# Strassen's scheme for a feed-forward up-projection, with a down-projection stage of its own

## The chip, the core and the metric

The kernel runs on one core of one Trainium2 chip. The metric is device time in microseconds (us) of one execution; the kernel before was timed three times: 2954.31, 2956.09 and 2958.66 us, median 2956.09.

## The reference

One layer of a streaming encoder on 512 tokens of width 2048, in float32. A mixer (a gated delta rule and a gated short convolution, between an input and an output projection) is followed by cross-attention into 256 memory tokens and by the feed-forward block that the change rewrites:

```python
def conv_ffn(h, w_up, conv_w, w_down):
    u = causal_dwconv(h @ w_up, conv_w)          # width 3, over tokens
    gate, up = u[..., :D_FF], u[..., D_FF:]      # D_FF = 5632
    return (jax.nn.silu(gate) * up) @ w_down
...
        h = rmsnorm(x, ffn_norm[l])
        x = x + conv_ffn(h, w_ffn_up[l], ffn_conv[l], w_ffn_down[l])
    return rmsnorm(x, final_norm)
```

## The kernel before, in words

Activations lie transposed: a tile of type T is [128 features, 512 tokens], and 16 of them hold one copy of the width. Every product of two float32 matrices is made of three matmuls (`mm3`, lines 149 to 152): each factor is split into a high and a low part of 12 significant bits in fp32r, and high x high, high x low and low x high are accumulated in PSUM. `wpiece` (line 131) loads a [128, 1024] piece of weights by SyncE's queue (tile wst, line 136), makes the high part on ScalarE (whi, line 139) and the low part on VectorE (wlo, line 140). `split` (lines 145 and 146) does the same for activations.

The stages follow one another: memory projections, mixer, attention scores, then `out_proj` (line 692), which brings attention's result back and adds it to the residual. There, tile by tile, ScalarE and GpSimd sum the squares for the norm, and the residual times the norm's gain is split into the high and low parts x2h and x2l (lines 710 and 711). The norm's factor of each token (`r2`) is applied after the up-projection, on its results.

The feed-forward block takes the 5632 hidden features in 11 chunks of 4 tiles (`FC`). For each of the 44 hidden tiles, `ffn_up` runs two projections (gate and up) of 16 k-tiles x 3 matmuls of 512 columns, multiplies by `r2` (line 729), does the convolution (lines 732 and 734), the Silu (736) and the product (737), and splits the result. `ffn_down` of the chunk before then adds this chunk's share of the down-projection to the residual tiles x2, which stay on chip (line 750). The last chunk goes through `ffn_down_last` in two halves of 256 tokens (line 766), each half with its final norm (lines 220, 211 to 216), its outputs (lines 782 to 785) and stores (787).

The order of instructions on each engine is not that of the program: a planner lets each engine take the earliest instruction of the program that it expects to be ready, and gives out the buffers of the pools. On the chip each engine then runs its instructions in that fixed order and waits on semaphores. Pools: `tp` (66 tiles of T), `wp` (3 wst, 4 whi, 4 wlo), `psm` and `psg` (3 and 5 banks of PSUM).

Of the kernel before, what the change touches and what calls it, by code (L numbers as in the profile page):

```python
# [15 lines left out]
P = 128  # L16
# [51 lines left out]
def trunk(ctx: ExitStack, tc: tile.TileContext, g):  # L68
    nc = tc.nc
    cpool = ctx.enter_context(tc.tile_pool(name="cpool", bufs=1))  # L70
    tp = ctx.enter_context(tc.tile_pool(name="tp", bufs=66))
    wp = ctx.enter_context(tc.tile_pool(name="wp", bufs=4))
# [10 lines left out]
    y_d = dpool.tile([H, P, S], F32, tag="y_d", name="y_d")  # L83
    gc_d = dpool.tile([4, H, P], F32, tag="gc_d", name="gc_d")
# [44 lines left out]
    def wpiece(src):  # L129
        """One [128, 1024] piece of weights, split into two parts of 12 significant bits."""  # L130
        st = wp.tile([P, 1024], F32, tag="wst", name=nm("wst"), bufs=3)
        shape = list(src.shape)
        stv = st
        if len(shape) == 3:
            stv = st.rearrange("p (a b) -> p a b", a=shape[1])
        nc.sync.dma_start(stv, src)
        hi = wp.tile([P, 1024], F32R, tag="whi", name=nm("whi"))
        lo = wp.tile([P, 1024], F32R, tag="wlo", name=nm("wlo"))
        nc.scalar.copy(hi, st)  # L139
        nc.vector.tensor_tensor(lo, st, f(hi), op=ALU.subtract)  # L140
        return hi, lo
# [40 lines left out]
    # the projections' pieces of weights, in order, split one piece ahead of their use  # L182
# [18 lines left out]
    def rsqrt(ms, ps, scale, bias):  # L201
        """1 / sqrt(ms), with one Newton step; ms = scale ps + bias is [128, n] in SBUF."""
# [20 lines left out]
    def rstd_rows(accs):  # L223
        """The norm's factor of each token, on every partition, from the sums of squares."""
# [43 lines left out]
    def mem_proj(w, then=None):  # L268
        """Projection of the normed memory, [hd, m], as two exact parts, two tiles of hd at a time."""
# [41 lines left out]
    # b and a of every head, the weights' two parts side by side  # L311
# [87 lines left out]
    def conv(ps, acc, c, taps):  # L399
        """Causal depthwise convolution over tokens, straight from PSUM."""  # L400
# [28 lines left out]
    def delta(h, q, k, v, z):  # L429
        q4, k4, v4_ = v4(q), v4(k), v4(v)  # L430
        # decays
# [12 lines left out]
        # k, tokens on partitions, and its norms: bk = beta / |k|^2, nk = |k|  # L444
# [17 lines left out]
        # k k^T and k q^T of each chunk  # L462
# [16 lines left out]
        # inverse of the unit triangular matrix: blocks of 32 by substitution,  # L479
        # a few columns of one block on each partition  # L480
# [36 lines left out]
        # then by blocks of doubling size: bt the inverse, pt its transpose  # L517
# [21 lines left out]
        # the scan over chunks  # L539
# [27 lines left out]
        # output norm (q's own norm is in it) and gate  # L567
# [72 lines left out]
    def turn():  # L640
        """The last softmax tiles, memory on partitions, as two exact parts."""
# [44 lines left out]
    x2, x2p = [], []  # L686
    x2s = []

    def out_proj(n, part):
        if part == 0:  # L690
            x2s.append((PM("psx2"), *wpiece(mo_d[:, :, n * P : (n + 1) * P].rearrange("k p n -> p k n"))))
        ps, hi, lo = x2s[n]
# [3 lines left out]
    for n in range(2):  # L696
        out_proj(n, 0)
    turn()
    for n in range(KT):
        if n >= 2:  # L700
            out_proj(n, 0)
        out_proj(n, 1)
        ps = x2s[n][0]
        x1 = T("x2")
        nc.sync.dma_start(x1, x1_d[n])
        nc.vector.tensor_tensor(x1, ps, x1, op=ALU.add)
        add_squares(acc2, x1, n == 0)
        th, tl = T("x2h", F32R), T("x2l", F32R)
        c = col(C_FFNN + n)
        nc.scalar.activation(th, x1, AF.Identity, scale=c)  # L710
        nc.vector.scalar_tensor_tensor(tl, x1, c, f(th), op0=ALU.mult, op1=ALU.subtract)
        x2.append(x1)
        x2p.append((th, tl))

# [1 line left out]
    r2 = []  # L716
    acc3 = cpool.tile([P, S], F32, tag="macc", name="acc3")

    def ffn_up(c):
        out = []  # L720
        for i in range(FC * c, FC * c + FC):
            us = []
            for t in (i, NF + i):
                ps = PM("psu")
                proj(lambda i2: g["w_up"][t, i2], x2p, ps)
                if not r2:
                    r2.append(rstd_rows([acc2]))
                u = T("u")
                nc.vector.tensor_tensor(u, ps, r2[0], op=ALU.mult)  # L729
                cv = T("ucv")  # L730
                cc = C_FCONV + 3 * t
                nc.scalar.activation(cv, u, AF.Identity, scale=col(cc + 2))
                for a in (1, 2):
                    nc.vector.scalar_tensor_tensor(cv[:, a:], u[:, : S - a], col(cc + 2 - a), cv[:, a:], op0=ALU.mult, op1=ALU.add)
                us.append(cv)
            nc.scalar.activation(us[0], us[0], AF.Silu)
            nc.vector.tensor_tensor(us[0], us[0], us[1], op=ALU.mult)
            out.append(split(us[0], "hd"))
        return out

    def ffn_down(c, hid):
        for n2 in range(KT // 2):
            hi, lo = wpiece(g["w_dn"][c, n2])
            for q in range(2):
                n = 2 * n2 + q
                ps = PG("psd")
                for k in range(FC):
                    o = k * 2 * P + q * P
                    mm3(ps, hi[:, o : o + P], lo[:, o : o + P], hid[k][0], hid[k][1], k == 0, k == FC - 1)
                nc.vector.tensor_tensor(x2[n], ps, x2[n], op=ALU.add)  # L750

    def ffn_down_last(c, hid):
        """The last part, the tokens in two halves, and the last norm of each."""
        S2 = S // 2
        for half in range(2):
            ts = slice(half * S2, (half + 1) * S2)
            for n2 in range(KT // 2):
                hi, lo = wpiece(g["w_dn"][c, n2])
                for q in range(2):
                    n = 2 * n2 + q  # L760
                    ps = PG("psd")[:, :S2]
                    for k in range(FC):
                        o = k * 2 * P + q * P
                        mm3(ps, hi[:, o : o + P], lo[:, o : o + P], hid[k][0][:, ts], hid[k][1][:, ts], k == 0, k == FC - 1)
                    xn = x2[n][:, ts]
                    nc.vector.tensor_tensor(xn, ps, xn, op=ALU.add)  # L766
                    if n == KT - 1:
                        last = T("sq")[:, :S2]
                        nc.scalar.activation(last, xn, AF.Square)
                    else:  # L770
                        add_squares(acc3[:, ts], xn, n == 0)
            r3 = rstd_rows([acc3[:, ts], last])
            if half == 0:
                nc.scalar.activation(cst[:, 3:4], r3[:, 0:1], AF.Ln)
            for n in range(KT):
                if n % 2 == 0:
                    o2 = T("o")
                o = o2[:, (n % 2) * S2 : (n % 2 + 1) * S2]
                xn = x2[n][:, ts]
                c2 = col(C_FINN + n)  # L780
                if n in (1, 4, 7, 9, 12, 14):
                    nc.scalar.activation(xn, xn, AF.Identity, scale=c2)
                    nc.gpsimd.tensor_tensor(o, xn, r3, op=ALU.mult)
                else:
                    nc.vector.scalar_tensor_tensor(o, xn, c2, r3, op0=ALU.mult, op1=ALU.mult)  # L785
                if n % 2:
                    nc.sync.dma_start(g["out"][n - 1 : n + 1, :, ts].rearrange("k p s -> p k s"), o2.rearrange("p (k s) -> p k s", k=2))

    prev = None
    for c in range(NF // FC):  # L790
        hid = ffn_up(c)
        if prev is not None:
            ffn_down(c - 1, prev)
        prev = hid
    ffn_down_last(NF // FC - 1, prev)


# [54 lines left out]
```

## Time and profile before

| What | Value |
|---|---|
| median of three executions | 2956.09 us |
| span of the profiled execution | 2963.6 us |
| TensorE, time in matmuls | 2901.9 us, 14497 matmuls |
| VectorE busy | 1551.5 us |
| ScalarE busy | 1053.6 us |
| GpSimd busy | 187.3 us |
| moved by the DMA engines | 365.42 MB, mean 123 GB/s |
| attention's output projection ends, up-projection begins | about 1500 us |

PE stands for TensorE, PEld for its weight loads, DVE for VectorE, ACT for ScalarE, POOL for GpSimd and SP for SyncE; L140 is line 140 of the kernel. A group's row gives engine, operation, output <- inputs with shapes, count, then busy time in us, mean duration in ns, and the engine's idle time just ahead of the group with what ended it. A row of stretches gives, from one time to another, each engine's busy time with its instructions, then the granted clock, the DMA engines' mean share and GB/s. A row of the timeline gives start and duration in us. A row of DMA issues ends with KB and the median us from issue to landing; a row of a DMA queue gives packets, MB and its packets' time as a share of 16 engines' span. Matmuls are pipelined, so what one costs is the distance from its start to the next one's.

### The profile page before, as it was taken

How to read it: one execution, taken by the hardware profiler on the slowest of the kernel's cores; microseconds unless marked ns; L12 is line 12 of the kernel's file. 1: busy time of each engine (PE TensorE's matmuls, PEld its weight loads, DVE VectorE, ACT ScalarE, POOL GpSimd, SP SyncE). 2: the span in 40 equal slices, each digit the busy share in tenths (PEclk: the TensorE clock that was granted, in tenths of full speed). 3: DMA queues.
4: the chain of work that ended last, by engine and by line, in shares of the span. 5: the costliest groups of instructions: out<-in, count | busy, mean ns of one | idle time of the engine just before them, and what ended most of it. 6: DMA issues, size and time to landing. Idle time of an engine off the chain costs nothing. (4 is left out here: it accounts for less than half of the span.)

```text
span 2963.6 us, 36108 instructions
## 1 busy us (share of the span) xinstructions
PE 2901.9 (98%) x14497; PEld 2437.6 (82%) x14497; DVE 1551.5 (52%) x2280; ACT 1053.6 (36%) x1427; POOL 187.3 (6%) x169
## 2 busy tenths in 40 slices
PE   7999999999999999999999999999999999999997
PEld 7999878777778888888888888888888888888887
DVE  5435747776664234446654544445454544444446
ACT  5454644444333223235443222223222232322225
POOL 1020001111110000110100000000000000000005
PEclk9999999999899999999999999999999999999999
DMA  6686763332232324446433333333333333333234
GB/s 201 214 287 199 237 192 107 89 96 82 82 96 87 100 94 152 148 147 185 143 113 94 99 99 93 100 95 97 100 93 99 98 94 100 94 98 100 93 100 135
DMA packets 143239, 365.42 MB, mean 123 GB/s; under 512 B 21200, under 2 KB 45152, under 8 KB 143072
## 3 DMA queue, kind: packets, MB, share of 16 engines
q1 hardware_dynamic: 129728, 337.93, 37.1%
q10 hardware_dynamic: 11392, 18.88, 1.7%
q0 software_dynamic: 1952, 6.31, 1.2%
q8 instruction: 113, 1.85, 0.2%
q14 instruction: 54, 0.44, 0.0%
HBM read 334.74 MB, written 28.33 MB: 123 GB/s over the span
## 5 line engine op out<-in xcount | busy, mean ns | idle before, releaser
L139 ACT CAST whi<-wst 128x1024 fp32r<-128x1024 f32 x592 | 622.1, 1052 | 1362.8 <-PE psu L151 472.9
L140 DVE TENSOR_TENSOR wlo<-wst,whi 128x1024 fp32r<-128x1024 f32 x592 | 726.2, 1228 | 601.3 <-ACT whi L139 577.7
L150 PE MATMUL psu<-x2h,whi 128*128 128x512 f32 x1408 | 548.1, 389 | 0.0
L152 PE MATMUL psu<-x2h,wlo 128*128 128x512 f32 x1408 | 547.7, 389 | 0.0
L151 PE MATMUL psu<-x2l,whi 128*128 128x512 f32 x1408 | 547.7, 389 | 0.0
L150 PEld LDWEIGHTS psu<-x2h,whi 128*128 128x128 f32 x1408 | 264.4, 188 | 55.1 <-issue 0.2
L151 PEld LDWEIGHTS psu<-x2l,whi 128*128 128x128 f32 x1408 | 264.4, 188 | 55.0 <-issue 0.2
L152 PEld LDWEIGHTS psu<-x2h,wlo 128*128 128x128 f32 x1408 | 264.3, 188 | 54.7
L150 PE MATMUL psd<-hdh,whi 128*128 128x512 f32 (+1 forms) x768 | 286.1, 373 | 2.7 <-DVE x L766 2.7
L152 PE MATMUL psd<-hdh,wlo 128*128 128x512 f32 (+1 forms) x768 | 286.2, 373 | 0.0
L151 PE MATMUL psd<-hdl,whi 128*128 128x512 f32 (+1 forms) x768 | 285.8, 372 | 0.0
L729 DVE TENSOR_TENSOR u<-psu,rsy 128x512 f32<-128x512 f32 x88 | 60.9, 692 | 288.8 <-PE psu L152 288.8
L750 DVE TENSOR_TENSOR x<-psd,x 128x512 f32<-128x512 f32 x160 | 110.7, 692 | 189.4 <-PE psd L152 189.4
L237 POOL TENSOR_TENSOR acc<-acc,sq 128x512 f32<-128x512 f32 (+1 forms) x58 | 73.4, 1266 | 1899.5 <-ACT sq L236 1898.3
L150 PEld LDWEIGHTS psd<-hdh,whi 128*128 128x128 f32 x768 | 145.4, 189 | 27.9 <-DVE x L766 2.9
L152 PEld LDWEIGHTS psd<-hdh,wlo 128*128 128x128 f32 x768 | 145.4, 189 | 25.0
L151 PEld LDWEIGHTS psd<-hdl,whi 128*128 128x128 f32 x768 | 145.4, 189 | 25.0
L150 PE MATMUL psq<-hh,whi 128*128 128x512 f32 x384 | 161.0, 419 | 0.0
L150 PE MATMUL psk<-mwh,whi 128*128 128x256 f32 x512 | 146.7, 286 | 12.5 <-ACT mwh L255 11.7
L151 PE MATMUL psq<-hl,whi 128*128 128x512 f32 x384 | 157.0, 409 | 0.0
L152 PE MATMUL psq<-hh,wlo 128*128 128x512 f32 x384 | 156.8, 408 | 0.0
L150 PE MATMUL pssc<-hh,whi 128*128 128x512 f32 x384 | 153.0, 398 | 0.0
(256 smaller groups left out, 4588.3 us busy)
## 6 DMA issues: line engine op xcount, KB each, us to landing
wst<-in_w_up SPq DMA_DIRECT2D x176, 512.0 KB, 3.5
wst<-in_w_mix SPq DMA_DIRECT2D x112, 512.0 KB, 3.6
wst<-in_w_dn SPq DMA_DIRECT2D x96, 512.0 KB, 3.5
wst<-in_w_xk SPq DMA_DIRECT2D x32, 512.0 KB, 3.6
wst<-in_w_xq SPq DMA_DIRECT2D x32, 512.0 KB, 4.5
wst<-in_w_xv SPq DMA_DIRECT2D x32, 512.0 KB, 4.3
wst<-in_w_xo SPq DMA_DIRECT2D x32, 512.0 KB, 4.7
wst<-in_w_mo SPq DMA_DIRECT2D x32, 512.0 KB, 3.6
```

The source lines that it names most:

```text
L139: nc.scalar.copy(hi, st)
L140: nc.vector.tensor_tensor(lo, st, f(hi), op=ALU.subtract)
L150: nc.tensor.matmul(ps, wh, xh, start=first, stop=False)
L151: nc.tensor.matmul(ps, wh, xl, start=False, stop=False)
L152: nc.tensor.matmul(ps, wl, xh, start=False, stop=last)
L237: nc.gpsimd.tensor_tensor(acc, acc, sq, op=ALU.add)
L729: nc.vector.tensor_tensor(u, ps, r2[0], op=ALU.mult)
L750: nc.vector.tensor_tensor(x2[n], ps, x2[n], op=ALU.add)
```

## The change

The up-projection is no longer 88 independent projections. For hidden tile i, the weights form a 2 x 2 block matrix: rows gate and up, columns the first and second half of the 2048 inputs (`w11`, `w12`, `w21`, `w22`, each [128, 1024]). The activations form another: the halves of the inputs by the halves of the tokens. One level of Strassen's scheme (with Winograd's sums) forms the four result blocks from 7 products of half-sized blocks in place of 8. The activations' sums are formed once, from pairs of residual tiles (n, n + 8) during the attention's output projection (`up_prepare`), and split: 7 operands of 8 k-tiles, 56 tiles of T. The weights' four sums are formed anew in each of the 44 units: `s1` and `s3` by accumulating DMAs from GpSimd's queue, `s2` and the last one on VectorE. PSUM accumulates px over products 1, 6, 7 and 4, and reads it out in between.

The residual x2 and the hidden tiles go through DRAM (`x2_d`, `hid_d`, written from ScalarE's queue). The down-projection follows as a stage of its own: four groups of four output tiles, each accumulating all chunks in PSUM, with the hidden tiles loaded and split again in each group. The last group leaves its last chunk out and does it in two halves of 256 tokens, with the final norm as before. Pools: `tp` 64 tiles, wst 5, whi and wlo 3 each; 7 residual work tiles (`tb`), whose place the 4 tiles of weight sums (`us`) take afterwards. The core of the diff:

```diff
+    def up_prepare(k, xa, xb):
+        tt = nc.vector.tensor_tensor
+        tc_, td = TB("tc"), TB("td")
+        tt(tc_[:, LO], xa[:, HI], xa[:, LO], op=ALU.subtract)
+        tt(tc_[:, HI], xb[:, HI], tc_[:, LO], op=ALU.subtract)
+        tt(td[:, LO], xa[:, HI], xb[:, HI], op=ALU.subtract)
+        tt(td[:, HI], xb[:, LO], tc_[:, HI], op=ALU.subtract)
...
+        for t, left, right in ((xb, 2, 3), (tc_, 5, 6), (td, 7, 4)):
+            th, tl = split(t, "xo")
+            xop[left].append((th[:, LO], tl[:, LO]))
+            xop[right].append((th[:, HI], tl[:, HI]))
...
+    for i in range(NF):
+        w11, w12, w21, w22 = (g["w_up"][q] for q in ((i, 0), (i, 1), (NF + i, 0), (NF + i, 1)))
+        s1 = us.tile([P, 1024], F32, tag="us", name=nm("s1"))
+        nc.sync.dma_start(s1, w21)
+        nc.gpsimd.dma_start(s1, w22, accum_op=ALU.add)
+        a11, a22, a12 = raw(w11), raw(w22), raw(w12)
+        s3 = us.tile([P, 1024], F32, tag="us", name=nm("s3"))
+        nc.scalar.activation(s3, a11, AF.Identity, scale=-1.0)
+        nc.gpsimd.dma_start(s3, w21, accum_op=ALU.add)
+        w1 = wsplit(a11)
+        px = PG("px")[:, :S2]
+        product(px, w1, 1, True)
+        tq, tz = T("tq"), T("tz")
+        nc.scalar.copy(tq[:, LO], px)
+        w2 = wsplit(a12)
+        py = PM("py")[:, :S2]
+        product(py, w2, 2, True)
+        tt(ug[:, LO], py, tq[:, LO], op=ALU.add)
+        s2 = us.tile([P, 1024], F32, tag="us", name=nm("s2"))
+        tt(s2, s1, a11, op=ALU.subtract)
+        product(px, wsplit(s2), 6, False)
+        nc.scalar.copy(tq[:, HI], px)
+        product(pz, wsplit(s1), 5, True)
+        nc.scalar.copy(tz[:, LO], pz)
+        product(px, wsplit(s3), 7, False)
+        tt(uu[:, HI], px, tz[:, LO], op=ALU.add)
+        tt(a12, a12, s2, op=ALU.subtract)
+        product(pz, wsplit(a12), 3, False)
+        tt(ug[:, HI], pz, tq[:, HI], op=ALU.add)
+        product(px, wsplit(a22), 4, False)
...
+        nc.scalar.dma_start(hid_d[i], cvs[0])
```

`product` runs 8 k-tiles x 3 matmuls of 256 columns; `wsplit` is the second half of `wpiece`, on a tile that is loaded already (`raw`).

More of the change, by code (lines that the diff above doesn't have):

```diff
@@ L83, in trunk @@
     y_d = dpool.tile([H, P, S], F32, tag="y_d", name="y_d")
+    x2_d = dpool.tile([KT, P, S], F32, tag="x2_d", name="x2_d")
+    hid_d = dpool.tile([NF, P, S], F32, tag="hid_d", name="hid_d")
     gc_d = dpool.tile([4, H, P], F32, tag="gc_d", name="gc_d")
@@ L129, in wpiece @@
     def wpiece(src):
-        st = wp.tile([P, 1024], F32, tag="wst", name=nm("wst"), bufs=3)
+        st = wp.tile([P, 1024], F32, tag="wst", name=nm("wst"), bufs=5)
         shape = list(src.shape)
@@ L691, in out_proj, with TB @@
             x2s.append((PM("psx2"), *wpiece(mo_d[:, :, n * P : (n + 1) * P].rearrange("k p n -> p k n"))))
-        ps, hi, lo = x2s[n]
+        ps, hi, lo = x2s[-1]
         for k in range(4 * part, 4 * part + 4):
             mm3(ps, hi[:, k * P : (k + 1) * P], lo[:, k * P : (k + 1) * P], *pp[k], k == 0, k == 7)
-    for n in range(2):
+    xop = {r: [] for r in (1, 2, 3, 4, 5, 6, 7)}
+    spool = ctx.enter_context(ExitStack())
+    tb = spool.enter_context(tc.tile_pool(name="tb", bufs=7))
+    def TB(s, dt=F32):
+        return tb.tile([P, S], dt, tag="tb", name=nm(s))
@@ L697, in trunk @@
+    turn()
+    xs1 = None
+    for idx in range(KT):
+        n = (idx % 2) * HK + idx // 2
         out_proj(n, 0)
[L698 to L701, printed above, removed]
         out_proj(n, 1)
-        ps = x2s[n][0]
-        x1 = T("x2")
+        ps = x2s[-1][0]
+        x1 = TB("x2")
         nc.sync.dma_start(x1, x1_d[n])
         nc.vector.tensor_tensor(x1, ps, x1, op=ALU.add)
[L707 to L713, printed above, removed]
@@ L716, in trunk, with raw @@
-    r2 = []
+        nc.scalar.dma_start(x2_d[n], x1)
+        add_squares(acc2, x1, idx == 0)
+        xs = TB("xs")
+        nc.scalar.activation(xs, x1, AF.Identity, scale=col(C_FFNN + n))
+        if idx % 2:
+            up_prepare(idx // 2, xs1, xs)
+        xs1 = xs
+    spool.close()
+    us = ctx.enter_context(tc.tile_pool(name="us", bufs=4, reuse_waits="tile"))
+    def raw(src):
+        t = wp.tile([P, 1024], F32, tag="wst", name=nm("wst"), bufs=5)
+        nc.sync.dma_start(t, src)
+        return t
@@ new lines, in wsplit, with product @@
+    def wsplit(t):
+        hi = wp.tile([P, 1024], F32R, tag="whi", name=nm("whi"))
+        lo = wp.tile([P, 1024], F32R, tag="wlo", name=nm("wlo"))
+        nc.scalar.copy(hi, t)
+        nc.vector.tensor_tensor(lo, t, f(hi), op=ALU.subtract)
+        return hi, lo
+    def product(ps, w, r, first):
+        hi, lo = w
+        for k in range(HK):
+            c = slice(k * P, (k + 1) * P)
+            xh, xl = xop[r][k]
+            nc.tensor.matmul(ps, hi[:, c], xh, start=first and k == 0, stop=False, skip_group_check=True)
+            nc.tensor.matmul(ps, hi[:, c], xl, start=False, stop=False, skip_group_check=True)
+            nc.tensor.matmul(ps, lo[:, c], xh, start=False, stop=k == HK - 1, skip_group_check=True)
@@ L717, in trunk, with hid_parts @@
+    NC_ = NF // FC
+    GN = 4
     acc3 = cpool.tile([P, S], F32, tag="macc", name="acc3")
-    def ffn_up(c):
+    x3 = []
+    def hid_parts(c):
         out = []
[L721 to L738, printed above, removed]
-        return out
@@ L741, in ffn_down @@
[L741 to L758, printed above, removed]
+        for k in range(FC):
+            t = T("hid")
+            nc.sync.dma_start(t, hid_d[c * FC + k])
+            out.append(split(t, "hd"))
@@ L759, in ffn_down_last, with bank @@
+        return out
+    def bank(gq, q):
+        return (PG if q < 2 or (q == 3 and gq % 2 == 0) else PM)("psd")
+    for gq in range(KT // GN):
+        last = gq == KT // GN - 1
+        pss = [bank(gq, q) for q in range(GN)]
+        nc_ = NC_ - 1 if last else NC_
+        for c in range(nc_):
+            hid = hid_parts(c)
+            for n2 in range(GN // 2):
+                hi, lo = wpiece(g["w_dn"][c, gq * GN // 2 + n2])
                 for q in range(2):
-                    n = 2 * n2 + q
@@ L772, in ffn_down_last @@
[L772 to L795, printed above, removed]
+                        mm3(pss[2 * n2 + q], hi[:, o : o + P], lo[:, o : o + P], *hid[k], c == 0 and k == 0, c == nc_ - 1 and k == FC - 1)
+        if last:
+            hid = hid_parts(nc_)
+        for q in range(GN):
+            n = gq * GN + q
+            x2 = T("x3")
+            nc.sync.dma_start(x2, x2_d[n])
+            nc.vector.tensor_tensor(x2, pss[q], x2, op=ALU.add)
+            x3.append(x2)
+            if not last:
+                add_squares(acc3, x2, n == 0)
@@ new lines, in trunk @@
+    wl = [wpiece(g["w_dn"][NC_ - 1, (KT - GN) // 2 + n2]) for n2 in range(GN // 2)]
+    for half in range(2):
+        ts = (LO, HI)[half]
+        for q in range(GN):
+            n = KT - GN + q
+            hi, lo = wl[q // 2]
+            ps = PG("psd")[:, :S2]
+            for k in range(FC):
+                o = k * 2 * P + (q % 2) * P
+                mm3(ps, hi[:, o : o + P], lo[:, o : o + P], hid[k][0][:, ts], hid[k][1][:, ts], k == 0, k == FC - 1)
+            xn = x3[n][:, ts]
+            nc.vector.tensor_tensor(xn, ps, xn, op=ALU.add)
+            if n == KT - 1:
+                sql = T("sq")[:, :S2]
+                nc.scalar.activation(sql, xn, AF.Square)
+            else:
+                add_squares(acc3[:, ts], xn, False)
+        r3 = rstd_rows([acc3[:, ts], sql])
+        if half == 0:
+            nc.scalar.activation(cst[:, 3:4], r3[:, 0:1], AF.Ln)
+        for n in range(KT):
+            if n % 2 == 0:
+                o2 = T("o")
+            o = o2[:, (n % 2) * S2 : (n % 2 + 1) * S2]
+            xn = x3[n][:, ts]
+            c2 = col(C_FINN + n)
+            if n in (1, 4, 7, 9, 12, 14):
+                nc.scalar.activation(xn, xn, AF.Identity, scale=c2)
+                nc.gpsimd.tensor_tensor(o, xn, r3, op=ALU.mult)
+            else:
+                nc.vector.scalar_tensor_tensor(o, xn, c2, r3, op0=ALU.mult, op1=ALU.mult)
+            if n % 2:
+                nc.sync.dma_start(g["out"][n - 1 : n + 1, :, ts].rearrange("k p s -> p k s"), o2.rearrange("p (k s) -> p k s", k=2))
```

43 lines of the change are left out of this document (31 added, 12 removed).

## The prediction

> **What bounds the kernel now.** I read the page from its head to the engines' shares, then the busy time by stretches, then the timeline where one matmul width follows the other.
>
> ```profile
> span 2963.6 us, 36108 instructions
> PE 2901.9 (98%) x14497; PEld 2437.6 (82%) x14497; DVE 1551.5 (52%) x2280; ACT 1053.6 (36%) x1427; POOL 187.3 (6%) x169
> ...
> core 0: us, PE busy (x) PEld busy (x) DVE busy (x) ACT busy (x) POOL busy (x), PEclk, DMA share, GB/s
> 150.00:200.00 50.00, 49.63 (x413) 49.42 (x413) 19.05 (x16) 30.52 (x41) 14.34 (x16) 1.00 0.88 293
> 450.00:500.00 50.00, 50.00 (x234) 41.67 (x233) 39.30 (x104) 19.96 (x33) 6.43 (x8) 1.00 0.37 104
> 1511.60:2893.70 1382.10, 1382.10 (x6098) 1144.60 (x6097) 666.74 (x769) 382.13 (x436) 0.00 (x0) 1.00 0.32 97
> 2917.00:2940.00 23.00, 19.27 (x143) 18.66 (x142) 19.95 (x30) 15.86 (x28) 13.53 (x15) 0.93 0.50 161
> ```
>
> TensorE is busy 2901.9 of 2963.6 us. From 1511.60 to 2893.70, nearly the whole feed-forward part, no gap is left and the granted clock is 1.00: 6098 matmuls of 512 columns in 1382.10 us, 0.2266 us each. VectorE is half busy there (666.74 us), the DMA engines carry a share of 0.32. So in this part time equals the number of matmuls times their spacing, and work for other engines costs only if it makes TensorE wait. The row 450 to 500 shows how far that reaches: VectorE at 39.30 of 50, 79%, and TensorE still full.
>
> ```profile
> 2893.48 0.39 PE L152 MATMUL psd<-hdh,wlo 128*128 128x512 f32 x1
> 2893.71 0.28 PE L150 MATMUL psd<-hdh,whi 128*128 128x256 f32 x1
> 2893.82 0.28 PE L151 MATMUL psd<-hdl,whi 128*128 128x256 f32 x1
> 2902.22 0.28 PE L152 MATMUL psd<-hdh,wlo 128*128 128x256 f32 x1
> ...
> 2893.71:2916.80 23.09, 23.09 (x194) 23.09 (x193) 6.83 (x16) 1.00 0.53 159
> ```
>
> The change needs the price of a matmul of half the width. Here the last chunk's token halves begin: the first 256-column matmul starts at 2893.71, 8.51 us and 71 starts later comes the one at 2902.22: 0.120 us each. (The window below has 194, two of them its edges; 16 tiles of 12 are 192.) Half the columns thus cost 53% of the time, and weight loads now fill the whole window (23.09 of 23.09).
>
> **The up-projection's matmuls.** Before, the groups of psu hold 3 x 1408 matmuls of 512 columns; those of psd 3 x 640 of 512 and 3 x 128 of 256.
>
> ```profile
> L150 PE MATMUL psu<-x2h,whi 128*128 128x512 f32 x1408 | 548.1, 389 | 0.0
> L150 PE MATMUL psd<-hdh,whi 128*128 128x512 f32 x640 | 249.0, 389 | 0.0
> L150 PE MATMUL psd<-hdh,whi 128*128 128x256 f32 x128 | 37.2, 290 | 2.7 <-DVE x L766 2.7
> ```
>
> After, each of 44 units runs 7 products x 8 k-tiles x 3 matmuls of 256 columns: 168, or 20.16 us; 7392 in all. 4224 x 0.2266 = 957.2 us become 7392 x 0.120 = 887.0: **-70.2**. One eighth fewer multiplications (-119.6) gives 49 back to the dearer narrow form. The Trainium skill (TensorE: Matmul & The Clock Gate, Back-to-back issue gap) puts the gap at N / 2.4 + 2.5 ns, which is 109.2 and 215.8 ns here and by my estimate a gain of 104 us. The rows of this kernel have both widths, 11 ns above it each, so they decide.
>
> **Down-projection.** It becomes 2064 x 512 and 96 x 256 columns: 467.7 + 11.5 = 479.2, against 435.1 + 46.1 = 481.2: **-2.0**. Its other work (four splits of hidden tiles and two of weights in 10.88 us) is 5.2 us on VectorE, hidden; its loads, 4 x 256 KB and 2 x 512 KB, are 2.1 MB in 10.88 us, 193 GB/s, below the 293 of the row 150 to 200.
>
> **VectorE and ScalarE in a unit.**
>
> ```profile
> L140 DVE TENSOR_TENSOR wlo<-wst,whi 128x1024 fp32r<-128x1024 f32 x592 | 726.2, 1228 | 601.3 <-ACT whi L139 577.7 <-DMA mk<-in_masks 7.4 <-PE psn L574 4.7
> L766 DVE TENSOR_TENSOR x<-psd,x 128x256 f32<-128x256 f32 x32 | 13.0, 418 | 7.0 <-PE psd L152 6.9
> L729 DVE TENSOR_TENSOR u<-psu,rsy 128x512 f32<-128x512 f32 x88 | 60.9, 692 | 288.8 <-PE psu L152 288.8
> L734 DVE SCALAR_TENSOR_TENSOR ucv<-u,cols,ucv 128x511 f32<-128x511 f32 x88 | 65.6, 745 | 0.0
> L737 DVE TENSOR_TENSOR ucv<-ucv,ucv 128x512 f32<-128x512 f32 x44 | 30.5, 692 | 1.5
> L711 DVE SCALAR_TENSOR_TENSOR x2l<-x,cols,x2h 128x512 fp32r<-128x512 f32 x16 | 20.4, 1278 | 20.2 <-ACT x2h L710 20.2
> L139 ACT CAST whi<-wst 128x1024 fp32r<-128x1024 f32 x592 | 622.1, 1052 | 1362.8 <-PE psu L151 472.9 <-PE psd L151 308.4 <-PE pssc L151 156.4
> L732 ACT ACTIVATE ucv<-u,cols 128x512 f32<-128x512 f32 x88 | 63.3, 719 | 1.2 <-DVE u L729 1.2
> L736 ACT ACTIVATE ucv<-ucv 128x512 f32<-128x512 f32 x44 | 27.8, 632 | 92.9 <-DVE ucv L734 92.9
> L236 ACT ACTIVATE sq<-x 128x256 f32<-128x256 f32 x28 | 11.0, 414 | 12.6 <-DVE x L766 12.6
> ```
>
> ```profile
> 2912.67 1.22 DVE L140 TENSOR_TENSOR wlo<-wst,whi 128x1024 fp32r<-128x1024 f32 x1 [1.06 <-ACT whi L139]
> 2913.82 0.75 DVE L766 TENSOR_TENSOR x<-psd,x 128x256 f32<-128x256 f32 x2
> ...
> ```
>
> VectorE per unit: seven low parts and two weight sums, 9 x 1.228 = 11.05; five operations on 256 columns (0.418 each), 2.09; one on 512, 0.69; four taps, 2.99; the product, 0.69. Together 17.5 us of 20.16. Back to back they overlap by some 0.08 us each (2912.67 + 1.22 against the next start at 2913.82), so 20 of them fill 15.9 us or 79%: just what the row 450 to 500 bore. ScalarE: 8 x 1.052 + 3 x 0.414 + 2 x 0.719 + 0.632 = 11.7 us. Both queues run in order. What must be prompt: px is read out by ScalarE (after products 1 and 6) or VectorE (after 7) while one other product of 2.88 us runs, and a split must end within the two products that three hi/lo buffers give, 5.76 us for about 2.5 us of work. What stands in a queue is one subtraction of 1.23 us at worst twice. I allow 0.25 us of waiting per unit, **+11**; bounds 0 and 0.6 (+26).
>
> **The adding DMAs.** No accumulating DMA is in the trace. The neighbours:
>
> ```profile
> wst<-in_w_up SPq DMA_DIRECT2D x176, 512.0 KB, 3.5
> x<-in_x POOLq DMA_DIRECT2D x16, 256.0 KB, 4.0
> gb<-gc_d POOLq DMA_DIRECT2D x8, 256.0 KB, 7.1
> q1 hardware_dynamic: 129728, 337.93, 37.1%
> q10 hardware_dynamic: 11392, 18.88, 1.7%
> q0 software_dynamic: 1952, 6.31, 1.2%
> 199.34 0.56 POOL L296 DMA_DIRECT2D x<-in_x  x1
> ...
> SPq L136 <- DVE wlo L140: 2264.7, 542, 12.4
> ```
>
> A plain 512 KB lands in 3.5 us, 256 KB from GpSimd's queue in 4.0, a finely cut one in 7.1. So one add of 512 KB lies between 3.5 and 2 x 7.1 = 14.2 us; I take 8.0, twice the row of the same queue and row shape. Two in a unit are 16 us even one behind the other, under 20.16, and they have lead: the sums' four buffers let the first sum load while the previous unit runs, and the second starts once the previous first sum is split, some 20 us before its use. On the 16 engines, q1 costs 0.371 x 2963.6 / 337.93 = 3.25 us per MB, q10 2.7, q0 5.6: four plain pieces 6.8, the hidden tile's write 0.7, two adds 5.9 if priced as q0, 11.8 if twice that: 13.4 to 19.3 of 20.16 us. Hidden, with little room. GpSimd's own part is 0.56 us an issue. SP's queue waits for buffers that VectorE frees (2264.7 us of it) and not for data, and so it will with the new loads, in unit order. Price taken: 0.
>
> **Stage borders.** The four sum buffers lie where the residual's work tiles were, and 16 tiles of probabilities plus 56 operand tiles exceed the 64 of the pool, so the last pairs are split only when the last attention product frees them. The first sum then needs: its buffer (3 to 6 us after the last attention matmul: the residual add, one scaling, four 0.42 us differences, up to three splits of 0.69), load 3.5, add 8.0, subtraction 1.2, cast 1.05; 16.8 to 19.8, of which products 1 and 2 hide 5.8: **+12**. Bounds: +3.5 (buffer free at once, add as quick as a load) and +20 (14.2 us add). VectorE's extra work beside the attention products (pairwise sums in place of the 1.28 us of x2l) fits: up to +5. Into the down stage the last unit's tail, store and reload stand ahead of chunk 10 only, which comes 109 us later: **+2** for the first splits (0 to 8).
>
> **The end.**
>
> ```profile
> 2925.98 8.32 DVE L785 SCALAR_TENSOR_TENSOR o<-x,cols,rsy 128x256 f32<-128x256 f32 x10
> 2946.32 0.28 PE L152 MATMUL psd<-hdh,wlo 128*128 128x256 f32 x1
> 2948.30 0.42 DVE L220 TENSOR_SCALAR ms<-psn 128x256 f32<-128x256 f32 x1 [1.24 <-PE psn L228]
> 2952.04 0.42 DVE L216 SCALAR_TENSOR_TENSOR rsy<-rst,rsy 128x256 f32<-128x256 f32 x1
> 2952.58 6.87 DVE L785 SCALAR_TENSOR_TENSOR o<-x,cols,rsy 128x256 f32<-128x256 f32 x10
> ```
>
> Before, 46.8 us lie between the end of half 0 (2916.80) and the end, 23.0 of them half 1's matmuls: 23.8 uncovered, partly the ten outputs of 8.32 us during which TensorE lost 3.7 us (row 2917 to 2940). After, half 1 is only 5.8 us of matmuls. From half 0's end: factor ready at +5.9 (2946.6 to 2952.5), outputs to +14.2, half 1's factor +4.3 (2948.30 to 2952.58), outputs and stores +11.0 (2952.58 to 2963.6): 29.5 less 5.8 is 23.7. **0**; bounds -8 (half 1's factor ahead of half 0's outputs) and +4.
>
> **The earlier stages** keep their instructions, but get two work tiles and one pair of split weights fewer and two raw weight tiles more. TensorE's idle time there is 61.7 us (2963.6 - 2901.9) less 17.0 after the last matmul and 3.7 in 2917 to 2940, so 41 us, partly where the DMA engines stand at 0.88 (row 150 to 200). More loads ahead and fewer splits ahead pull to opposite sides: **0**, with a quarter of the 41 either way, 10.
>
> Sum: -70.2 - 2.0 + 11 + 12 + 2 = -47.2, so 2963.6 becomes 2916.4. The profiled execution is 7.5 us above the median of 2956.09; I take the same off: **2909**. With its bounds this case reaches from 2870 (-70.2 - 2.0 - 8 + 3.5 - 10 = -86.7) to 2947 (-72.2 + 26 + 20 + 8 + 5 + 4 = -9).
>
> **Rivals.**
> *VectorE's queue takes over (to slower, or nearly).* If 79% were the most it can do in order and its instructions did not overlap, a unit would take 17.5 / 0.79 = 22.2 us: 44 x 2.0 = 88 instead of my 11, so 2986. It decides from 1.32 us of loss per unit, where 2909 - 11 + 58 meets 2956. For it: x2l took 1.28 us for a kind that costs 0.75 elsewhere (row L734), while GpSimd added squares, so neighbours can stretch VectorE. Against: GpSimd does no arithmetic in the new loop, and 79% was borne at 450 to 500. A milder form, 0.6 to 1 us, ends at 2924 to 2942.
> *The adds become the bound (slower).* Two serial adds of 14.2 us make a unit of 28.4 us: 44 x 8.2 = 363 more, less the allowance: 3261. It decides from 10.7 us per add. For it: 19.3 of 20.16 us on the engines by the upper price. Against: rows of 2 KB took 4.0. The Trainium skill (Collectives: The Full Stack, The bandwidth ceiling) says that an adding transfer reads two sources and so runs at half the rate; that is the upper price, 19.3, and alone would not yet bind.
> *Nothing is lost.* Queues and start hide all: 2956.1 - 72.2 = 2884.
>
> **Chances.** Forecast 0.62, VectorE's queue 0.17, adds 0.11, nothing lost 0.10. This kernel's runs can tell 0.2% (6 us) from no change. Faster: 0.62 + 0.10 and a small part of the second, 0.74; within 0.2%: 0.05 from the second's milder end; slower 0.21. The range 2870 to 2962 holds the first and last cases and the milder second.
>
> **What would show it.** Products on px, py, pz starting 0.120 us apart, some 20.4 us from one unit to the next; VectorE near 80% between; the adds landing in about 8 us; one gap of some 12 us before the first unit's third product; about 24 us after half 1's last matmul. Wrong if units are over 21.5 us apart: then the wait in front of TensorE names VectorE (second case) or the DMA behind a sum (third).

## The result, and the profile after

The changed kernel takes 3151.98 us (median of four, 3137.80 to 3159.05) against 2957.38 us for the kernel before: 1.0644 times as long, 95% interval 1.061 to 1.0679. The forecast was 2909 us; even its upper end, 2962, is 190 us short. The head of the page after, and its rows of DMA queues and of the chain that ended last:

```profile
span 3145.6 us, 44069 instructions
PE 2912.0 (93%) x17521; PEld 2548.8 (81%) x17521; DVE 1821.9 (58%) x2680; ACT 1346.1 (43%) x1879; POOL 256.4 (8%) x246
...
q0 software_dynamic: 14624, 52.45, 9.5%
...
PE 56%; DMA 7%; DVE 3%; ACT 3%; issue 2%; SPq 0%; POOL 0%; DVEq 0%; ACTq 0%; POOLq 0%
```

Before, TensorE was busy for 98% of the span; after, for 93%, and 7% of the chain that ended last are DMAs. Where the time went shows in the busy time by stretches (stretch, PE, PEld, DVE, ACT, POOL, granted clock, DMA share, GB/s):

```profile
1500.00:1520.00 20.00, 6.97 (x31) 6.27 (x30) 8.24 (x9) 5.08 (x7) 3.53 (x4) 0.58 0.77 174
1600.00:1700.00 100.00, 100.00 (x836) 100.00 (x835) 81.47 (x100) 54.67 (x70) 7.88 (x10) 1.00 0.65 172
2200.00:2300.00 100.00, 100.00 (x836) 100.00 (x835) 81.47 (x100) 54.65 (x69) 8.60 (x10) 1.00 0.66 171
2420.00:2820.00 400.00, 309.93 (x1152) 230.94 (x1151) 124.02 (x153) 109.91 (x158) 9.74 (x7) 0.90 0.39 131
```

The first row is the start of the up-projection, the next two are its body: TensorE is full, 836 matmuls in 100 us, VectorE at 81%. This stage begins at about 1494 us and ends at about 2400, 906 us. The last row is the down-projection, and there the loss lies. It holds 1152 matmuls, 24 chunks of 48, in 400 us: 16.67 us a chunk instead of 48 x 0.2266 = 10.88. Of the 139 us lost in the row, 90.1 are idle TensorE (400 - 309.93); the other 48.9 are matmuls that count as busy for longer than 0.2266 us (309.93 - 1152 x 0.2266). By the starts in the trace some 37 us of these are matmuls that follow one another late with no wait between, at a mean granted clock of 0.90; the rest stands at the 68 waits of the row, where the matmul ahead counts its 0.39 us instead of 0.23. The row holds two of the three borders between groups of output tiles, with waits of 10.42 and 11.90 us; the nine chunks from 2608.83 to 2753.19, between them, take 16.04 us each. Over 43 chunks 5.79 us make 249 us, an estimate. The whole stage, from 2400 to the end, takes 745.6 us; the forecast for it and the tail was 2 + 479.2 + 23.7 = 505, so it is some 241 us over.

What ended the waits of that stage (us in total, times, longest), and how a chunk runs in the timeline (SyncE, then ScalarE, then TensorE):

```profile
ACT hdh L147 <- DMA hid<-hid_d: 248.8, 44, 7.0
ACT whi L141 <- PE psd L153: 241.7, 43, 11.3
...
PEld psd L152 <- ACT hdh L147: 180.6, 82, 12.3
...
PE psd L152 <- ACT hdh L147: 146.8, 77, 11.9
```

```profile
2600.93 2.07 SPq L138 DMA_DIRECT2D wst<-in_w_dn  x2
2603.33 2.65 SPq L834 DMA_DIRECT2D hid<-hid_d  x4
2617.45 2.07 SPq L138 DMA_DIRECT2D wst<-in_w_dn  x2
2619.57 1.85 SPq L834 DMA_DIRECT2D hid<-hid_d  x4
```

```profile
2600.17 1.05 ACT L141 CAST whi<-wst 128x1024 fp32r<-128x1024 f32 x1
2601.13 0.61 ACT L147 CAST hdh<-hid 128x512 fp32r<-128x512 f32 x1
2608.16 1.28 ACT L147 CAST hdh<-hid 128x512 fp32r<-128x512 f32 x2 [6.42 <-DMA hid<-hid_d]
```

```profile
2608.83 2.01 PE L152 MATMUL psd<-hdh,whi 128*128 128x512 f32 x4 [2.44 <-ACT hdh L147]
...
2611.50 0.63 PE L153 MATMUL psd<-hdl,whi 128*128 128x512 f32 x1
2611.92 0.59 PE L154 MATMUL psd<-hdh,wlo 128*128 128x512 f32 x1
2612.35 0.40 PE L153 MATMUL psd<-hdl,whi 128*128 128x512 f32 x1
2612.59 0.40 PE L154 MATMUL psd<-hdh,wlo 128*128 128x512 f32 x1
```

Read it backwards. TensorE starts on the next hidden tiles at 2608.83, when ScalarE has cast them; ScalarE got them at 2608.16, 6.42 us after its last work; SyncE issued them from 2603.33 on, right behind two weight pieces. In the instruction order of SyncE's queue the two weight pieces of chunk c + 4 stand ahead of the last two hidden tiles of chunk c + 1 and the first two of chunk c + 2. A weight piece needs one of 5 raw buffers; that is free once an earlier piece has been split; a split needs one of 3 pairs of whi and wlo; a pair is free once TensorE is through with a piece of chunk c. So the weights run some three chunks ahead, and the hidden tiles, which wait for nothing that matters, are issued behind them when TensorE has almost nothing left to do. Each chunk then pays for a hidden load (5.4 us, the second row of DMA issues below) and a split, less what is left to compute.

```profile
s<-in_w_up POOLq DMA_DIRECT2D x88, 512.0 KB, 6.4
...
hid<-hid_d SPq DMA_DIRECT2D x176, 256.0 KB, 5.4
```

The theory put to the test: the order in the in-order queues makes the loss, not the amount of loads or splits. Its rivals: too few split buffers; the reload's own price; the new up-projection and its adding DMAs working into the next stage; the accumulators changing in PSUM at the borders between groups.

### The profile page after: what moved, and what is told of

The parts are those of the page before. It is cut to its first block, busy times and chain, and to the rows that moved or that the text cites. A ratio compares the mean times of both kernels' runs of the same rounds, so it can differ in the third digit from the quotient of the medians.

```text
span 3145.6 us, 44069 instructions
## 1 busy us (share of the span) xinstructions
PE 2912.0 (93%) x17521; PEld 2548.8 (81%) x17521; DVE 1821.9 (58%) x2680; ACT 1346.1 (43%) x1879; POOL 256.4 (8%) x246
## 3 DMA queue, kind: packets, MB, share of 16 engines
q1 hardware_dynamic: 156224, 384.08, 37.1%
## 4 chain that ended last, share of the span: by engine, by line
PE 56%; DMA 7%; DVE 3%; ACT 3%; issue 2%; SPq 0%; POOL 0%; DVEq 0%; ACTq 0%; POOLq 0%
DMA hid<-hid_d 6%; PE px L772 5%; PE px L770 5%; PE px L771 5%; PE psd L152 4%; PE psd L153 3%; PE psx L153 3%; PE psx L154 3%; PE psx L152 3%; PE psd L154 3%; PE pz L772 3%; PE pz L770 3%; PE pz L771 3%; PE pssc L152 3%; PE pssc L154 3%; PE pssc L153 2%
## 5 line engine op out<-in xcount | busy, mean ns | idle before, releaser
L770 PE MATMUL px<-xoh,whi 128*128 128x256 f32 x1056 | 300.2, 284 | 13.2 <-ACT whi L760 12.9
L771 PE MATMUL px<-xol,whi 128*128 128x256 f32 x1056 | 299.9, 284 | 0.0
L772 PE MATMUL px<-xoh,wlo 128*128 128x256 f32 x1056 | 299.9, 284 | 0.0
L770 PEld LDWEIGHTS px<-xoh,whi 128*128 128x128 f32 x1056 | 203.8, 193 | 13.6 <-ACT whi L760 13.1
L147 ACT CAST hdh<-hid 128x512 fp32r<-128x512 f32 x176 | 106.8, 616 | 250.2 <-DMA hid<-hid_d 248.8
L771 PEld LDWEIGHTS px<-xol,whi 128*128 128x128 f32 x1056 | 203.8, 193 | 0.0
L772 PEld LDWEIGHTS px<-xoh,wlo 128*128 128x128 f32 x1056 | 203.8, 193 | 0.0
L772 PE MATMUL pz<-xoh,wlo 128*128 128x256 f32 x704 | 199.4, 283 | 0.9 <-DVE wlo L761 0.9
L770 PE MATMUL pz<-xoh,whi 128*128 128x256 f32 x704 | 199.5, 283 | 0.2 <-ACT whi L760 0.2
L771 PE MATMUL pz<-xol,whi 128*128 128x256 f32 x704 | 199.3, 283 | 0.0
L760 ACT CAST whi<-s 128x1024 fp32r<-128x1024 f32 x132 | 138.2, 1049 | 96.1 <-PE px L771 64.3
```

The source lines that it names most:

```text
L147: nc.scalar.copy(th, t)
L760: nc.scalar.copy(hi, t)
L770: nc.tensor.matmul(ps, hi[:, c], xh, start=first and k == 0, stop=False, skip_group_check=True)
L771: nc.tensor.matmul(ps, hi[:, c], xl, start=False, stop=False, skip_group_check=True)
L772: nc.tensor.matmul(ps, lo[:, c], xh, start=False, stop=k == HK - 1, skip_group_check=True)
```

## The experiments

### The hidden tiles' loads on GpSimd's queue

```diff
-            nc.sync.dma_start(t, hid_d[c * FC + k])
+            nc.gpsimd.dma_start(t, hid_d[c * FC + k])
```

> Edit: the loads of the hidden tiles are issued from GpSimd's queue instead of SP's. Theory A (queue order): in SP's queue those loads stand behind weight loads for chunks up to three ahead, which wait for a raw buffer, so for a low part, so for a hi/lo buffer that only TensorE frees; a hidden tile therefore starts to load only when the chunk before it is half done. Taken out of that queue they land early, a chunk goes from about 16.05 us back to 10.88, 43 x 5.2 = 222 us and some clock come back: 2905 to 2935 us. Theory B (the trip through DRAM or the three hi/lo buffers set the pace, whatever the queue): 3100 to 3160, no change.

3073.33 us, 1.0392 times before (1.0367 to 1.0417): between the two. ScalarE's waits for hidden loads fall from 248.8 to 14.9 us, yet a chunk away from the borders still takes 13.28 us, against 16.04. ScalarE's queue, in the timeline:

```profile
2616.69 1.99 ACT L141 CAST whi<-wst 128x1024 fp32r<-128x1024 f32 x2 [9.20 <-PE psd L153]
2618.59 2.17 ACT L147 CAST hdh<-hid 128x512 fp32r<-128x512 f32 x4
```

The four splits, whose data has long landed, stand behind two weight casts that wait 9.20 us for TensorE. It is the same pattern in a second queue: the loads had only hidden it. TensorE then waits for the first of the four splits:

```profile
2619.26 1.21 PE L152 MATMUL psd<-hdh,whi 128*128 128x512 f32 x4 [1.47 <-ACT hdh L147]
```

The Trainium skill (DMA: Bandwidth & Descriptors, Issuing engines are not separate DMA queues) says that spreading DMAs over issuing engines saves only the sequencer's time to start them. Here it saved 79 us, since it let the loads pass a queue that was blocked.

### Four pairs of split weights instead of three

```diff
-    wp = ctx.enter_context(tc.tile_pool(name="wp", bufs=3))
+    wp = ctx.enter_context(tc.tile_pool(name="wp", bufs=4))
```

and raw weight buffers 3 instead of 5, for the room.

> Edit: 4 hi and 4 lo buffers with 3 raw ones, as before the change, in place of 3 and 5 (same bytes); hidden tiles still on SP. Theory A: a weight load still waits for TensorE seven pieces back instead of eight, and the planner keeps the hidden loads behind it, so a chunk stays near 16 us: 3110 to 3190. Theory B (too few hi/lo buffers): chunks near 10.9 us, 2925 to 2960.

3192.37 us (one run): the rival falls. With three raw buffers and four pairs a weight piece waits for TensorE seven pieces back instead of eight, and in SyncE's order the hidden tiles still stand behind weight pieces for two or three chunks later. More pairs without fewer raw buffers were not tried.

### The hidden tiles' loads one chunk earlier

```diff
+            hid_load()                  # the four loads of chunk c + 1, on SyncE
             hid = hid_parts(c)          # only the splits of chunk c
```

> Edit: the loads of the hidden tiles stay on SP but stand one chunk earlier in the program. Theory A: they then stand ahead of the weight loads that wait for the same chunk, land in time and a chunk takes near 10.9 us: 2905 to 2950. Theory B (the trip through DRAM is the bound): no change, 3100 to 3160.

2937.44 us (one run): 215 us of the loss are gone, with the same loads and splits on the same queues. Away from the borders the hidden tiles of chunk c now stand ahead of the second weight piece of chunk c in SyncE's order. The same stretch as above:

```profile
2420.00:2820.00 400.00, 384.82 (x1664) 316.20 (x1663) 183.10 (x229) 161.17 (x235) 15.00 (x11) 0.98 0.56 194
```

1664 matmuls instead of 1152. What TensorE still waits for splits, from 2400 us on, is four waits, one at the stage's start and one at each of the three borders between the groups of four output tiles:

```profile
PE psd L152 <- ACT hdh L147: 19.2, 4, 5.6
```

### The down stage alone, with the up-projection of before

The kernel before, with only the residual and the hidden tiles through DRAM and the down stage of its own.

> Edit on the kernel before: no Strassen, the up-projection and its buffers (66 tiles, 3 raw, 4 hi, 4 lo) as before; only residual and hidden tiles through DRAM and the down-projection as its own stage, hidden loads on SP. Theory A: the stage by itself brings the loss, 2956 - 2 + 222 = about 3176 (3130 to 3200). Theory C (the loss comes from the two parts together, by the 56 operand tiles or the three hi/lo buffers): 2950 to 2975.

3193.47 us (one run). Between 2500 and 2900 us it has 1154 matmuls, against the changed kernel's 1152 in its own 400 us:

```profile
2500.00:2900.00 400.00, 310.96 (x1154) 231.88 (x1155) 125.21 (x153) 110.80 (x160) 9.75 (x7) 0.90 0.39 132
```

This kernel loses 236 us against the one before without Strassen's scheme and without adding DMAs: the loss comes with the down stage.

### The same with the loads one chunk earlier

> The kernel of before with only the residual and the hidden tiles through DRAM and the down stage of its own (3193), and the hidden tiles' loads one chunk ahead. Theory A (a down stage whose loads are ahead costs nothing but its borders, -2 + 2 and about 5 us at each of three borders, so that Strassen's up-projection is worth some 20 us less than nothing is lost, about 55 to 60 us net of its start gap): 2960 to 2990. Rival B (the down stage still loses more than its borders when the up-projection is the old one): 3000 and above.

2984.81 us (one run), as the theory has it: 29 us above the kernel before (2955.85, timed beside it), of which 19.7 are waits for the first splits at the stage's start and at the borders. Against this kernel, 2937.44 with the new up-projection is 47 us less, on single runs, where 55 to 60 were expected.

### Loads and splits one chunk earlier

```diff
+    ahead2 = [hid_parts(todo.pop(0))]
...
-            hid = hid_parts(c)
+            hid = ahead2.pop(0)
+            if todo:
+                ahead2.append(hid_parts(todo.pop(0)))
```

(`todo` holds the chunk numbers of all four groups in order.)

> The changed kernel, with the hidden tiles of a chunk loaded and split one chunk earlier in program order, all on SyncE's queue as it was, same work and same bytes. Theory A (the order of SyncE's and ScalarE's queues makes the loss: the hidden tiles' loads and splits stand behind weight pieces that wait for TensorE): the chunk goes from 16.05 us back to about 10.9, time 2905 to 2960. Rival B (the down stage's loads or splits are too many in whatever order): 3100 to 3160. Rival C (only half of it is order, the other half the reload's own time): 3000 to 3080.

3146.69 us, 1.0639 times before (1.0613 to 1.0666): no change. It seems to speak for the rival, but SyncE's order came out the same, load by load: two weight pieces of chunk c + 4, then the four hidden tiles. The planner orders by what it expects to be ready, and writing the step earlier did not move it. So this kernel tests nothing but that a place in the program isn't a place in a queue.

### All weight sums on VectorE

The loads-ahead kernel, without the two adding DMAs of a unit and ScalarE's negated copy:

```diff
-        nc.gpsimd.dma_start(s1, w22, accum_op=ALU.add)
-        nc.scalar.activation(s3, a11, AF.Identity, scale=-1.0)
-        nc.gpsimd.dma_start(s3, w21, accum_op=ALU.add)
+        tt(s3, s1, a11, op=ALU.subtract)
+        tt(s1, s1, a22, op=ALU.add)
```

> The kernel with the hidden tiles' loads one chunk ahead (2937), and all four weight sums of a unit on VectorE: the adding DMAs and ScalarE's negated copy are gone, VectorE gets two sums of 1.23 us more per unit, some 91% of 20.16 us instead of 79 to 81%. Theory A (VectorE's queue has room to 90%, and the adding DMAs bring nothing here): 2927 to 2947. Rival B (above 80 to 85% the in-order queue makes TensorE wait, so the adding DMAs carry part of the up-projection's gain): 1 to 2 us per unit, 2980 to 3030.

2931.29 us (one run), inside the first theory's band. The body of the up-projection:

```profile
1600.00:1700.00 100.00, 100.00 (x835) 100.00 (x835) 92.41 (x110) 49.48 (x64) 0.00 (x0) 1.00 0.33 118
```

VectorE at 92.41% still leaves TensorE no gap, and the DMA share is half of the 0.65 of after. The adding DMAs cover nothing here. At the first unit the wait is 8.9 us, against 14.0 with the adds.

### The hidden tiles in the sums' buffers, and the first sum in a raw-weight buffer

Both start from the loads-ahead kernel; the second has both edits.

```diff
-            raws.append([T("hid") for _ in range(FC)])
+            raws.append([us.tile([P, 1024], F32, tag="us", name=nm("hid")) for _ in range(FC // 2)])
```

> As the kernel with the hidden tiles' loads one chunk ahead (2937), but the raw hidden tiles lie two by two in the four buffers of the weight sums, which are idle in the down stage, and come in two DMAs of 512 KB per chunk. Theory A (what is left of the loss is the hidden tiles' loads waiting at the three borders of tile groups for buffers that TensorE's operands hold): 2915 to 2935. Rival B (what is left is TensorE's accumulators changing at the borders): 2932 to 2942, as before.

```diff
-        s1 = us.tile([P, 1024], F32, tag="us", name=nm("s1"))
+        s1 = us.tile([P, 1024], F32, tag="us", name=nm("s1")) if i else wp.tile([P, 1024], F32, tag="wst", name=nm("wst"), bufs=5)
```

> As the kernel with the hidden tiles in the sums' buffers, and the first unit's first sum in a raw-weight buffer instead of a buffer that the residual's work tiles must free. Theory A (the gap of 12.9 us ahead of the first unit's third product is the wait for that buffer, then load, add, subtraction, split): the gap shrinks to 3 to 6 us, and the time is 7 to 12 us below that of the kernel that differs only in this. Rival B (the gap is the operands of the residual's last pairs, which free late): no change, within 3 us.

2932.91 us (0.9915 times before, 0.9896 to 0.9933) and 2928.39 us (0.9897 times, 0.9882 to 0.9911). The first lies in both bands; its row from 2600 to 2700 is still 94.93% busy, so the buffers were not what the borders wait for. The second's waits of TensorE at the start are:

```profile
PE pz L772 <- DVE wlo L761: 3.9, 2, 3.0
PE px L770 <- ACT whi L760: 3.2, 1, 3.2
PE px L770 <- ACT tq L798: 1.2, 1, 1.2
```

The gap of 14.4 us in the first shrank to 3.2, as the theory has it, but some 4.5 us of it came back as smaller waits behind. The time is 4.5 us lower, less than the theory's 7 to 12 and more than the rival's 3, and the intervals of the two ratios overlap.

### The same without adding DMAs

The kernel of 2928.39 with the sums on VectorE, as in the diff above.

> The kernel with the hidden tiles in the sums' buffers and the first sum in a raw-weight buffer (2928) with one edit: all four weight sums of a unit on VectorE, no adding DMA and no negated copy on ScalarE. Theory A (the adding DMAs bring nothing at 81% of VectorE, and cost only time at the first unit, where an add of some 6 us stands ahead of the first sums): 2920 to 2929. Rival B (at 92% VectorE's queue makes TensorE wait now and then): 2932 to 2960.

2924.13 us (0.99 times before, 0.9869 to 0.9931). Not slower than with the adds; whether faster can't be told.

### The next group's splits ahead of the squares

At a border ScalarE's queue held the last weight casts and the group's four squares, each waiting for a result of TensorE, ahead of the next group's first hidden cast. The kernel of 2924 with three edits in the order of the program:

```diff
+        for q in range(GN):                       # at the group's start
+            x3.append(T("x3"))
+            nc.sync.dma_start(x3[-1], x2_d[gq * GN + q])
...
-            hid = hid_parts(c)
+            hid = parts.pop(0)                    # split one chunk earlier
+            if raws:
+                parts.append(hid_parts(c))
+            if c == 2:                            # the squares of the group before
+                while late:
+                    n = late.pop(0)
+                    add_squares(acc3, x3[n], n == 0)
```

(`hid_parts` takes the next loaded chunk, whatever its argument; the loads stand two chunks ahead here.)

> The kernel with the hidden tiles in the sums' buffers and the first sum in a raw-weight buffer (2928), with three more edits: the four weight sums on VectorE, no adding DMA; the residual's tiles of a group of outputs loaded at the group's start; the splits of hidden tiles one chunk earlier, and a group's four squares two chunks later in the program, which puts the splits of two chunks of the next group ahead of these squares and of the last weight pieces in ScalarE's queue. Theory A (the 4.4 us gaps at the three group borders, with the lower clock behind them some 5 us each, are the next group's first split standing behind the squares and weight pieces in ScalarE's queue): they vanish, 2905 to 2918. Rival B (the borders cost this because TensorE's accumulators change there): 2922 to 2932.

2906.63 us, 0.9829 times before (0.9809 to 0.985). The stretch of the down stage, then TensorE's waits from 1400 us to the end of the matmuls:

```profile
2420.00:2820.00 400.00, 400.00 (x1767) 331.20 (x1766) 203.26 (x243) 177.01 (x250) 16.96 (x11) 1.00 0.61 207
```

```profile
PE psn L230 <- POOL acc L239: 7.5, 2, 6.8
PE px L770 <- ACT whi L760: 5.8, 1, 5.8
PE psd L152 <- ACT hdh L147: 2.7, 1, 2.7
```

1767 matmuls, those cut by the row's two ends among them, in 400 us are 0.2264 us each: with the three borders inside, TensorE never waits, and the same loads and splits lie hidden at a DMA share of 0.61. The rival that PSUM costs at the borders falls. The one wait for a split that is left is at the stage's start.

Without the earlier splits:

> The fastest kernel so far (2907) without one of its edits: the splits of hidden tiles are back at their own chunk in the program; the squares of a group stay two chunks late. Counted in the order of ScalarE's queue, the splits of two chunks of the next group still stand ahead of the squares and of the last weight pieces. Theory A (only the order in ScalarE's queue counts, and the late squares alone made it): 2903 to 2911, no gap at the borders. Rival B (the splits must be written a chunk early too): 2915 to 2925, gaps of 4 us at the borders.

2908.91 us, 0.9821 times before (0.9805 to 0.9837). The stretches with the three borders are full:

```profile
2500.00:2600.00 100.00, 100.00 (x443) 82.81 (x442) 53.37 (x65) 46.53 (x67) 4.83 (x3) 1.00 0.60 207
2600.00:2700.00 100.00, 100.00 (x443) 82.81 (x442) 48.14 (x57) 42.01 (x60) 6.06 (x4) 1.00 0.58 199
2700.00:2800.00 100.00, 100.00 (x443) 82.81 (x442) 49.02 (x58) 43.81 (x61) 6.05 (x4) 1.00 0.58 199
```

The late squares with the early residual loads made it (which of the two is not shown); the earlier splits add nothing. This is the simpler of the two fastest versions.

## Why the prediction was wrong, point by point

**The step that failed** is the one on the down-projection: "Its other work (four splits of hidden tiles and two of weights in 10.88 us) is 5.2 us on VectorE, hidden; its loads ... 193 GB/s, below the 293", and with it the matmul sum of -2.0 as the stage's whole price. Both numbers are right, and they answer another question. They compare amounts with capacities; the stage was bound by order, with VectorE at 31% (124.02 of 400) and the DMA engines at 0.39. I walked through the queues for the up-projection and for the border, not for a chunk of the down stage, where six loads of two kinds with different reuse of buffers share SyncE's queue. Instead of 0 the step cost some 240 us. None of the rivals had it: two sought the danger in the up-projection, and the third saw none. The "+2 for the first splits (0 to 8)" was no part of the failure: TensorE waits 4.53 us between the two stages.

**Up-projection, -70.2**: right. From 1600 to 2390 us 6583 matmuls start, 0.1200 us apart (forecast 0.120), so 7392 are 887 us. On single runs the new up-projection is worth 47 us net, and the forecast was -70.2 + 11 + 12 = -47. That they agree is in part luck: the 11 did not come, and the start cost more than 12, as the next points show.

**VectorE, +11**: the 79% was nearly right (81.47), the waiting was not there: the body has no gap, and none at 92% either. The rival that VectorE's queue takes over does not hold here up to that load.

**The adding DMAs, 0**: right for the body; they land in 6.4 us (forecast 8.0, between 3.5 and 14.2). Their packets cost more than those of queue q1, which are 0.371 x 3145.6 / 384.08 = 3.0 us per MB after: q0 went from 1.2% to 9.5% of the span for 46.14 MB more, 0.095 x 3145.6 less 0.012 x 2963.6 is 263 us, 5.7 us per MB. But the row of q0 before, without adding, said 5.6 already, so the price is that queue's here, and no doubling by the adding, the prediction's upper price, shows.

**The start, +12**: right in place, too small in size. The timeline has the wait ahead of the first unit's third product, and the row of stretches below it has the granted clock at 0.50:

```profile
1513.59 0.58 PE L770 MATMUL px<-xoh,whi 128*128 128x256 f32 x1 [12.88 <-ACT whi L760]
```

```profile
1510.00:1520.00 10.00, 6.25 (x27) 5.96 (x28) 6.99 (x6) 4.05 (x5) 0.87 (x1) 0.50 0.65 145
```

From its first to its last matmul the stage takes 905.7 us, some 19 more than the 887: the wait of 12.88, the lower clock behind it (some 3 us) and smaller losses. The forecast had priced the wait alone; the 19 lies within its bounds. The wait has two causes of like size, as the experiments show: the buffer that comes free late, and the adds. All of TensorE's waits at the start together are 14.3 to 15.8 us with neither edit, 10.5 without the adds, 9.1 with the other buffer, 7.5 with both.

**The earlier stages, 0**: within the 10 allowed. The first matmul of the up-projection starts at 1493.95 us, against 1500.17 before. (The prediction's upper end, -9, leaves these 10 us out where its lower end counts them; with them it would be 2957, which changes nothing in the account.)

**The tail, 0**: nearly. 26.2 us lie between half 1's last matmul and the end after (23.7 forecast, 24.2 in the kernel of 2906.63).

**The sum** of -47 is what the change is worth once the order is mended: 2906.63 us is 49 below the kernel before that was timed beside it. That is a sum of other terms, though: the waits at the start are half as long there, VectorE costs nothing, and there are no adding DMAs. So the nearness is luck, and the blind number was right for a kernel that was not the one under test.

## What to carry to other kernels

A stage is hidden only if each load is also issued in time: walk through every in-order queue of a new stage, instruction by instruction, and ask what each one waits for and what stands behind it. Here two streams shared a queue, and the deeper buffered one blocked the other, for it waited on the consumer while the other had nothing to wait for; a fourth pair of split buffers, at the price of two raw ones, did not help (3192.37 us). Moving the stream to another queue shows whether the next queue has the same order, and a change in the program counts only when the queues' order has changed.

## What was not expected of the hardware

- The clock falls after short gaps. Away from the borders the chunks of the changed kernel's down stage have one gap of TensorE of 1.5 to 3.0 us each (2.44 in the timeline above) besides gaps below 1 us, and behind most of them matmuls of 512 columns started 0.43 us apart for some 3.5 us (2608.83 to 2612.35 in the timeline above), then 0.23. Between 2420 and 2820 us the granted clock is at half in 15 such stretches of 3.41 us, and in two of 13.65 us behind the border waits of 10.42 and 11.90. This took about a quarter of the loss there (some 37 of 139 us). The Trainium skill (TensorE: Matmul & The Clock Gate, HAM oscillation) warns of gaps over about 3.4 us; here gaps of at most 3.0 us that recur every 16 us were enough. The Trainium skill (TensorE: Matmul & The Clock Gate, Wait — 56ns, not 53.3ns?) gives 426.7 ns for the lower clock at this width, which agrees with the 0.43.
- VectorE bore 92.41% of busy time in an in-order queue that feeds TensorE, with no gap in 100 us.
